# Weight splits of the feed-forward in whole granules without GpSimd's share, and token lists from signs on ScalarE

## The chip, the cores and the metric

The kernel runs on one core of one Trainium2 chip. The metric is the device time of one launch in microseconds (us). The engines are named as the profile names them: PE is TensorE, DVE is VectorE, ACT is ScalarE, POOL is GpSimd, SP is SyncE, which issues most of the DMAs. "L0" and "L1" below are the two layers of the model, while L88 or L343 is a line of the kernel's file.

## What is computed

A diffusion backbone of two layers over 1024 tokens of 1024 channels. Each layer has a mixer (a gated DeltaNet with pooling in the first, a short convolution in the second) and then a feed-forward with 16 experts, in which each expert chooses its 128 tokens. The change touches the feed-forward alone:

```python
def expert_choice_ffn(h, router, w_gate, w_up, w_down):
    b, n, _ = h.shape                                   # 1, 1024
    cap = EC_CAPACITY_FACTOR * n // N_EXPERTS           # 2 * 1024 // 16 = 128
    aff = jax.nn.softmax(jnp.einsum('bnd,de->bne', h, router).astype(jnp.float32), axis=-1)
    gate, idx = lax.top_k(aff.transpose(0, 2, 1), cap)  # each expert's 128 best tokens
    bidx = jnp.arange(b)[:, None, None]
    xg = h[bidx, idx]
    hid = jax.nn.silu(jnp.einsum('becd,edf->becf', xg, w_gate)) * jnp.einsum('becd,edf->becf', xg, w_up)
    y = jnp.einsum('becf,efd->becd', hid, w_down) * gate[..., None].astype(h.dtype)
    return jnp.zeros_like(h).at[bidx, idx].add(y)
```

An expert's weights are two matrices of 1024 x 512 and one of 512 x 1024, all float32: 6 MB an expert, 96 MB a layer.

## The kernel before

**Weights.** Products are made in three passes with operands split into a high part (float32r) and a low part. Weights come from DRAM in granules of 1 MB, 128 partitions x 4 x 512 = 2048 columns. For each granule ACT copies the raw float32 to the high part (whi, L87) and DVE or POOL subtracts to get the low part (wlo, L88). `Weights.split` does so in two halves of 1024 columns, and hands every sixth half to POOL (`pool_share=6`), the others to DVE. An expert has six granules: gate and up for each half of its inputs, then two of down. There are 8 buffers for raw granules and 6 pairs for split ones, taken in turns; SP issues the next load once a raw buffer is free.

**Selection.** `Moe.select` finds each expert's 128th best value by ten rounds of a search. In a round DVE counts on all 1024 tokens (junk), compares (ok, L303), PE sums over partitions (pn, L305), and DVE sets the new candidate; in the first seven rounds this takes an addition of two columns of SBUF (cbase, L308) beside it. Then dg (L315), pth and th spread the threshold, m (L322, L323) marks the tokens above it and equal to it, and 16 matmuls into pp count the marks ahead of each token: one with a triangular matrix, seven with ones for the tiles of tokens ahead, and eight that add the total of the greater ones to the equal ones. Two DVE operations make slot of it, each token's place in each expert's list, or 0.

**Lists and rows.** `Moe.gather` makes an expert's list: a one-hot oh of 8 tiles x 128 places on DVE (L343), eight matmuls of it with the tokens' numbers (pi, L351), a copy to int32 on ACT (idx, L354), then POOL issues the indirect DMA that gathers the rows (xg, L356), and ACT copies the expert's weight of each row out of them (aff, L359). Rows are transposed by PE and split by ACT and DVE (xh, xl).

**Experts.** `Moe.experts` gathers for three experts ahead, prefetches six granules behind the selection, up to four of them with the subtraction on POOL (behind `self.routed`, the last tile's softmax) and the rest on DVE (behind `self.placed`, the last list made so far), then loops over the 16 experts: gather for the third next one, products with gate and up (gu, L139 to L141), silu and product, products with down (py), the result times its weight (y, L454), and an indirect DMA on POOL's queue that adds it to acc in DRAM (L459).

The stage of the experts runs in L0 from the selection at 707.6 us to the last y at 1079.4, in L1 from 1494.9 to 1875.9. What goes on which engine is written in the code; the order of instructions on each engine is set by the scheduler of the framework from priorities, dependences and modelled times, not by the order of the code.

## Time and profile before

| | |
|---|---|
| device time, median of 3 runs | 1914.73 us (1910.54 to 1923.18) |
| span of the profiled execution | 1906.9 us, 26387 instructions |
| PE busy | 1669.8 us (88%) |
| DVE busy | 1373.4 us (72%) |
| ACT busy | 843.1 us (44%) |
| POOL busy | 689.6 us (36%) |
| moved by DMA | 443.73 MB, 233 GB/s in the mean |
| splits on DVE (L88), all shapes | 370, 511.9 us |
| splits on POOL (L88), all shapes | 90, 244.8 us |

The profiled execution has no time of its own beside its span; the span is 7.8 us shorter than the median of the runs. Shares of busy time are means over the whole program. The feed-forward takes about 40% of it, in two stretches, and is read by itself in the rows below.

### The profile page before, as it was taken

The numbers are of one execution on the slowest core, as the hardware profiler recorded it, in microseconds if no ns is written. First come the engines' busy times: TensorE is split into PE (matmuls) and PEld (weight loads), VectorE is DVE, ScalarE is ACT, GpSimd is POOL, SyncE is SP. The second block draws the span as 40 slices with busy tenths as digits, with TensorE's granted clock in tenths as the row PEclk, the third lists the DMA queues.
The fourth block names the chain that finished last, engine by engine and source line by source line (L and its number), as shares of the span: only waits on it lengthen the run. The fifth ranks groups of instructions, "written<-read, shape, count | busy, mean of one in ns | idle before, by whom it ended". The sixth has DMA issues, their size and how long they took to land. (4 is left out here: it accounts for less than half of the span.)

```text
span 1906.9 us, 26387 instructions
## 1 busy us (share of the span) xinstructions
PE 1669.8 (88%) x9561; PEld 1352.4 (71%) x9561; DVE 1373.4 (72%) x2128; ACT 843.1 (44%) x1503; POOL 689.6 (36%) x614
## 2 busy tenths in 40 slices
PE   5999996989979874999998899999999388999995
PEld 3988774767867663777776677888888267777673
DVE  4637777666887866999988858523635688888896
ACT  3644332425642333677665451111222256566673
POOL 3310377551240344444442360000022546454423
PEclk8999998979989886999999999999999689999998
DMA  7425774558768946999998648403354479999975
GB/s 293 135 96 185 229 197 140 149 176 248 241 224 275 349 174 211 333 372 352 349 357 278 209 137 321 132 20 127 133 186 142 176 239 315 350 320 336 349 254 198
DMA packets 261400, 443.73 MB, mean 233 GB/s; under 512 B 46521, under 2 KB 108714, under 8 KB 257174
## 3 DMA queue, kind: packets, MB, share of 16 engines
q1 hardware_dynamic: 252198, 408.76, 62.1%
q0 software_dynamic: 9072, 33.30, 7.2%
q8 instruction: 75, 1.23, 0.3%
q14 instruction: 55, 0.45, 0.1%
HBM read 368.65 MB, written 73.35 MB: 232 GB/s over the span
## 5 line engine op out<-in xcount | busy, mean ns | idle before, releaser
L88 DVE TENSOR_TENSOR wlo<-raw,whi 128x1024 fp32r<-128x1024 f32 (+2 forms) x370 | 511.9, 1426 | 59.1 <-ACT whi L87 59.0
L87 ACT CAST whi<-raw 128x1024 fp32r<-128x1024 f32 (+2 forms) x460 | 438.5, 1021 | 213.4 <-PE pin L140 77.7
L88 POOL TENSOR_TENSOR wlo<-raw,whi 128x1024 fp32r<-128x1024 f32 (+1 forms) x90 | 244.8, 2730 | 337.2 <-ACT whi L87 310.2
L140 PE MATMUL gu<-wlo,xh 128*128 128x512 f32 x512 | 210.3, 411 | 22.8 <-DVE wlo L88 18.7
L139 PE MATMUL gu<-whi,xh 128*128 128x512 f32 x512 | 207.7, 410 | 7.2 <-ACT whi L87 7.1
L141 PE MATMUL gu<-whi,xl 128*128 128x512 f32 x512 | 206.5, 405 | 0.0
L141 PE MATMUL pin<-h1T,wlo 128*128 128x512 f32 x384 | 150.2, 392 | 0.7 <-POOL wlo L88 0.7
L140 PE MATMUL pin<-h1T,whi 128*128 128x512 f32 x384 | 150.7, 393 | 0.0
L139 PE MATMUL pin<-h1T,whi 128*128 128x512 f32 x384 | 148.9, 395 | 0.0
L459 POOL DMA_INDIRECT acc<-y,idx x31 | 85.3, 2750 | 149.6 <-DVE y L454 133.2
L140 PEld LDWEIGHTS gu<-wlo,xh 128*128 128x128 f32 x512 | 99.3, 194 | 53.2 <-DVE wlo L88 26.0
L139 PEld LDWEIGHTS gu<-whi,xh 128*128 128x128 f32 x512 | 99.4, 194 | 32.9 <-ACT whi L87 10.0
L141 PEld LDWEIGHTS gu<-whi,xl 128*128 128x128 f32 x512 | 98.9, 193 | 21.7
L449 PE MATMUL py<-whi,hh 128*128 128x512 f32 x256 | 108.0, 422 | 4.7 <-ACT idx L354 2.6
L785 DVE SCALAR_TENSOR_TENSOR adsum<-raw,cs,adsum 128x512 f32<-128x512 f32 (+1 forms) x77 | 96.6, 1255 | 21.4 <-DMA raw<-in_ada_w_dram 21.0
L449 PE MATMUL py<-wlo,hh 128*128 128x512 f32 x256 | 107.0, 418 | 0.0
L139 PE MATMUL pq<-hT,whi 128*128 128x512 f32 (+1 forms) x256 | 97.7, 382 | 1.8 <-ACT last L1079 1.3
L139 PE MATMUL po<-whi,mh 128*128 128x512 f32 x224 | 92.2, 413 | 6.6 <-DVE ox L611 6.6
L141 PE MATMUL pq<-hT,wlo 128*128 128x512 f32 (+1 forms) x256 | 97.5, 381 | 0.0
L140 PE MATMUL pq<-hT,whi 128*128 128x512 f32 (+1 forms) x256 | 97.0, 379 | 0.0
L140 PE MATMUL po<-wlo,mh 128*128 128x512 f32 x224 | 91.3, 408 | 5.8 <-DVE wlo L88 5.8
L141 PE MATMUL po<-whi,ml 128*128 128x512 f32 x224 | 90.8, 406 | 0.0
(385 smaller groups left out, 3652.4 us busy)
## 6 DMA issues: line engine op xcount, KB each, us to landing
raw<-in_w_gate_dram SPq DMA_DIRECT2D x64, 1024.0 KB
raw<-in_w_up_dram SPq DMA_DIRECT2D x64, 1024.0 KB
raw<-in_w_down_dram SPq DMA_DIRECT2D x64, 1024.0 KB
raw<-in_ada_w_dram SPq DMA_DIRECT2D x32, 1024.0 KB
raw<-in_ada_w_dram SPq DMA_DIRECT2D x64, 256.0 KB
raw<-in_sc_w_in_dram SPq DMA_DIRECT2D x12, 1024.0 KB
table<-h SPq DMA_DIRECT2D x16, 520.0 KB
raw<-in_ev_w_in_dram SPq DMA_DIRECT2D x16, 512.0 KB
```

Source lines behind the costliest of these rows:

```text
L87: nc.scalar.copy(hi[:, part], raw[:, part])
L88: (lo_engine or e).tensor_sub(lo[:, part], raw[:, part], hi[:, part])
L139: nc.tensor.matmul(out, lhs[0], rhs[0], start=start, stop=False)
L140: nc.tensor.matmul(out, lhs[0], rhs[1], start=False, stop=False)
L141: nc.tensor.matmul(out, lhs[1], rhs[0], start=False, stop=stop)
L449: nc.tensor.matmul(py, hh[:, k, :], g[w][:, k, :], start=k == w == 0, stop=False)
L459: self.scattered = nc.gpsimd.indirect_dma_start(out=self.acc[:, :], out_offset=bass.IndirectOffsetOnAxis(ap=idx, axis=0), in_=y, in_offset ...
L785: nc.vector.scalar_tensor_tensor(st["sum"], raw, cs[:, k, 0:1], st["sum"], op0=ALU.mult, op1=ALU.add)
```

## The change

The feed-forward's weights are split in one piece of 2048 columns a granule (`parts=1`), and no piece goes to POOL by turn (`pool_share=0`). The prefetch that names POOL as its engine still goes there. The two other users of `Weights` in this stretch of the program (the early prefetch in layer 0, the output projection in layer 1) keep halves.

The lists are no longer made from slots. With the count of an expert's chosen tokens up to and with each token, a place p of the list belongs to the first token whose count is over p. So the number of the token at place p is the number of tokens whose count is not over p, and that is a sum of signs: ACT takes, for each of the 8 tiles of tokens, the sign of (p + 0.5 - count) with the count as its bias per partition, PE sums the signs over tokens by products with a column of ones, and ACT makes 0.5 x sum + 512 of it, the token's number. Counts are of the greater tokens plus the equal ones up to what is left of the 128 places. That takes the total of the greater ones (pg, eight matmuls of 16 columns), in place of the eight matmuls that added it to the equal ones, and three DVE operations on small tiles in place of two. The counts overwrite the affinities' tile (`self.before = aff`), and `self.placed` is now the last of those three operations.

```diff
 class Weights:
-    def __init__(self, co, raw, pool, size=GRAN, pool_share=6):
+    def __init__(self, co, raw, pool, size=GRAN, pool_share=6, parts=2):
 ...
+        self.parts = parts
 ...
-        n = raw.shape[1] // 2
-        for part in (slice(0, n), slice(n, 2 * n)):
+        n = raw.shape[1] // self.parts
+        for part in (slice(i * n, (i + 1) * n) for i in range(self.parts)):
 def route_constants(co, c, tmp):
-    co.iota1 = c.tile([P, P], F16, name="iota1")
-    nc.gpsimd.iota(co.iota1, pattern=[[1, P]], base=1, channel_multiplier=0, ...)
-    co.tokid = c.tile([P, NT], F16, name="tokid")
-    nc.gpsimd.iota(co.tokid, pattern=[[P, NT]], base=0, channel_multiplier=1, ...)
+    co.places = c.tile([P, P], F16, name="places")
+    nc.gpsimd.iota(co.places, pattern=[[1, P]], base=0, channel_multiplier=0, ...)
+    nc.vector.tensor_scalar(co.places, co.places, 0.5, None, op0=ALU.add)
 ...
+    co.ones16 = c.tile([P, 1], F16, name="ones16")
+    nc.vector.memset(co.ones16, 1.0)
 class Moe:
     def select(self, pool, ps):
 ...
+        pg = ps.tile([P, 512], F32, tag="tr", name=co.name("pg"))
+        for t in range(NT):
+            nc.tensor.matmul(pg[:, :NE], co.one16, m[:, 0, t, :], start=t == 0, stop=t == NT - 1)
         nc.tensor.matmul(pp[:, : 2 * NT * NE], co.tri16, m.rearrange("p m t e -> p (m t e)"), start=True, stop=False)
         for j in range(1, NT):
-            nc.tensor.matmul(pp4[:, :, j:, :], co.one16, m[:, :, : NT - j, :], start=False, stop=False)
-        for t in range(NT):
-            nc.tensor.matmul(
-                pp4[:, 1], co.one16, m[:, 0, t : t + 1, :].to_broadcast([P, NT, NE]), start=False, stop=t == NT - 1
-            )
-        self.slot = self.rp.tile([P, NT, NE], F16, name=f"slot{self.li}")
-        s1 = pool.tile([P, 2, NT, NE], F32, tag="junk", name=co.name("s1"), bufs=1)
-        nc.vector.tensor_tensor(s1, pp4, m, op=ALU.mult)
-        nc.vector.tensor_tensor(self.slot, s1[:, 0], s1[:, 1], op=ALU.add)
+            nc.tensor.matmul(pp4[:, :, j:, :], co.one16, m[:, :, : NT - j, :], start=False, stop=j == NT - 1)
+        left = pool.tile([P, 1, NE], F32, tag="left", name=co.name("left"), bufs=1)
+        nc.vector.tensor_scalar(left[:, 0, :], pg[:, :NE], -1.0, float(CAP), op0=ALU.mult, op1=ALU.add)
+        equal = pool.tile([P, NT, NE], F32, tag="junk", name=co.name("equal"), bufs=1)
+        nc.vector.tensor_tensor(equal, pp4[:, 1], left.to_broadcast([P, NT, NE]), op=ALU.min)
+        self.before = aff
+        self.placed = nc.vector.scalar_tensor_tensor(
+            flat(self.before), pp[:, : NT * NE], -1.0, flat(equal), op0=ALU.mult, op1=ALU.subtract
+        ).ins
     def gather(self, e, pool, ps):
         oh = pool.tile([P, NT, P], F16, tag="oh", name=co.name("oh"), bufs=2)
-        self.placed = nc.vector.tensor_tensor(
-            oh, self.slot[:, :, e : e + 1].to_broadcast([P, NT, P]),
-            co.iota1.rearrange("p (o s) -> p o s", o=1).to_broadcast([P, NT, P]), op=ALU.is_equal,
-        ).ins
         pi = ps.tile([P, 512], F32, tag="tr", name=co.name("pi"))
         for t in range(NT):
-            nc.tensor.matmul(pi[:, :1], oh[:, t, :], co.tokid[:, t : t + 1], start=t == 0, stop=t == NT - 1)
+            nc.scalar.activation(oh[:, t, :], co.places, AF.Sign, bias=self.before[:, t, e : e + 1])
+            nc.tensor.matmul(pi[:, :1], oh[:, t, :], co.ones16, start=t == 0, stop=t == NT - 1)
 ...
-        nc.scalar.copy(idx, pi[:, :1])
+        nc.scalar.activation(idx, pi[:, :1], AF.Copy, scale=0.5, bias=float(SEQ // 2))
 def feed_forward(li, ready, start, before_last):
-            weights = Weights(co, Cycle((raws_on, n_raw), *(...)), Cycle(*splits))
+            weights = Weights(co, Cycle((raws_on, n_raw), *(...)), Cycle(*splits), pool_share=0, parts=1)
```

The changed file's line numbers are higher by one to five. Three places of the order show what moved. The numbers behind tiles' names count tiles; "x8" is eight instructions in a row. First ACT, in layer 0, from the last granule that is prefetched (raw_7479) to the first expert's rows. Before:

```order
L87 CAST whi_7866<-raw_7479 128x1024 x2
L354 CAST idx_7790<-pi_7781 128x1
L354 CAST idx_7807<-pi_7798 128x1
L354 CAST idx_7824<-pi_7815 128x1
L359 COPY aff_7791<-xg_7793 128x1
L133 CAST xh_7835<-pt_7830 128x512
```

And with the change (raw_7480 is the same granule, aff_6918 holds the counts):

```order
L88 CAST whi_7884<-raw_7480 128x2048
L353 ACTIVATE oh_7782<-places,aff_6918 128x128 x8
L353 ACTIVATE oh_7806<-places,aff_6918 128x128 x8
L357 ACTIVATE idx_7800<-pi_7783 128x1
L353 ACTIVATE oh_7830<-places,aff_6918 128x128 x8
L357 ACTIVATE idx_7824<-pi_7807 128x1
L353 ACTIVATE oh_7888<-places,aff_6918 128x128 x8
L357 ACTIVATE idx_7848<-pi_7831 128x1
L353 ACTIVATE oh_8022<-places,aff_6918 128x128 x7
L362 COPY aff_7801<-xg_7803 128x1
L353 ACTIVATE oh_8022<-places,aff_6918 128x128
L134 CAST xh_7859<-pt_7854 128x512
```

The first list's copy to idx stands behind the signs of two experts, and the first copy out of a gathered row behind those of five.

Second POOL, from the end of the last tile's modulation (h, on both) through the prefetch to the first scatter. Before:

```order
L284 TENSOR_TENSOR h_7644<-h_7644,bc_6889 128x1024
L88 TENSOR_TENSOR wlo_7849<-raw_7293,whi_7848 128x1024 x2
L88 TENSOR_TENSOR wlo_7855<-raw_7295,whi_7854 128x1024 x2
L88 TENSOR_TENSOR wlo_7861<-raw_7387,whi_7860 128x1024 x2
L88 TENSOR_TENSOR wlo_7867<-raw_7479,whi_7866 128x1024 x2
L356 DMA xg_7793<-table_73,idx_7790 128x1040
L356 DMA xg_7810<-table_73,idx_7807 128x1040
L356 DMA xg_7827<-table_73,idx_7824 128x1040
L356 DMA xg_7886<-table_73,idx_7883 128x1040
L88 TENSOR_TENSOR wlo_8059<-raw_8056,whi_8058 128x1024
L88 TENSOR_TENSOR wlo_8234<-raw_8231,whi_8233 128x1024
L356 DMA xg_8013<-table_73,idx_8010 128x1040
```

And with the change:

```order
L285 TENSOR_TENSOR h_7645<-h_7645,bc_6890 128x1024
L89 TENSOR_TENSOR wlo_7873<-raw_7294,whi_7872 128x2048
L89 TENSOR_TENSOR wlo_7877<-raw_7296,whi_7876 128x2048
L89 TENSOR_TENSOR wlo_7881<-raw_7388,whi_7880 128x2048
L89 TENSOR_TENSOR wlo_7885<-raw_7480,whi_7884 128x2048
L359 DMA xg_7803<-table_73,idx_7800 128x1040
L359 DMA xg_7827<-table_73,idx_7824 128x1040
L359 DMA xg_7851<-table_73,idx_7848 128x1040
L359 DMA xg_7909<-table_73,idx_7906 128x1040
L359 DMA xg_8043<-table_73,idx_8040 128x1040
L462 DMA acc_75<-y_7992,idx_7800 1024x1024
```

The four prefetched granules stay on POOL, in four pieces where there were eight; the single pieces between the gathers are gone.

Third DVE, from the end of the search (dg) to the first splits of the loop. Before:

```order
L315 TENSOR_SCALAR dg_7744<-ident,cand_7678 128x16
L319 COPY th_7748<-pth_7746 128x16
L322 TENSOR_TENSOR m_7750<-aff_6917,th_7748 128x128
L323 TENSOR_TENSOR m_7750<-aff_6917,th_7748 128x128
L336 TENSOR_TENSOR s_7771<-pp_7753,m_7750 128x256
L337 TENSOR_TENSOR slot_7770<-s_7771 128x128
L343 TENSOR_TENSOR oh_7779<-slot_7770,iota_6503 128x1024
L343 TENSOR_TENSOR oh_7796<-slot_7770,iota_6503 128x1024
L343 TENSOR_TENSOR oh_7813<-slot_7770,iota_6503 128x1024
L343 TENSOR_TENSOR oh_7872<-slot_7770,iota_6503 128x1024
L343 TENSOR_TENSOR oh_7999<-slot_7770,iota_6503 128x1024
L134 TENSOR_TENSOR xl_7836<-pt_7830,xh_7835 128x512
```

And with the change:

```order
L316 TENSOR_SCALAR dg_7745<-ident,cand_7679 128x16
L320 COPY th_7749<-pth_7747 128x16
L323 TENSOR_TENSOR m_7751<-aff_6918,th_7749 128x128
L324 TENSOR_TENSOR m_7751<-aff_6918,th_7749 128x128
L336 TENSOR_SCALAR left_7772<-pg_7755 128x16
L338 TENSOR_TENSOR equal_7774<-pp_7754,left_7772 128x128
L342 SCALAR_TENSOR_TENSOR aff_6918<-pp_7754,equal_7774 128x128
L135 TENSOR_TENSOR xl_7860<-pt_7854,xh_7859 128x512
L135 TENSOR_TENSOR xl_7869<-pt_7863,xh_7868 128x512
L135 TENSOR_TENSOR xl_7918<-pt_7912,xh_7917 128x512
L89 TENSOR_TENSOR wlo_8069<-raw_8066,whi_8068 128x2048
```

Five one-hots are gone between slot and the first rows. The ten rounds ahead of dg, with the seven additions of cbase in them, stand as they did.

## Rows read from the trace of the kernel before

**Rows 1.** Busy time by stretch, the middles of both layers; columns in the first line.

```profile
core 0: us, PE busy (x) PEld busy (x) DVE busy (x) ACT busy (x) POOL busy (x), PEclk, DMA share, GB/s
770.00:1038.00 268.00, 247.09 (x1171) 195.91 (x1170) 252.83 (x215) 176.58 (x228) 116.22 (x52) 0.97 1.01 345
1600.00:1840.00 240.00, 219.72 (x1010) 172.85 (x1009) 214.29 (x187) 151.18 (x194) 114.67 (x45) 0.94 1.00 340
```

**Rows 2.** The same view, four shorter stretches of the middles.

```profile
870.00:920.00 50.00, 48.80 (x237) 38.92 (x235) 48.55 (x44) 34.08 (x44) 18.67 (x9) 1.00 1.04 367
920.00:970.00 50.00, 46.11 (x223) 36.78 (x224) 48.22 (x41) 34.42 (x46) 23.17 (x12) 0.97 1.05 356
...
1600.00:1640.00 40.00, 35.80 (x173) 28.55 (x171) 40.00 (x32) 26.41 (x34) 26.95 (x9) 0.96 1.03 368
1640.00:1680.00 40.00, 37.60 (x172) 29.52 (x173) 29.66 (x31) 22.94 (x29) 13.80 (x7) 0.91 0.91 308
```

**Rows 3.** Groups by line, 747:1080 (layer 0): count, busy, mean ns, idle before.

```profile
L88 DVE TENSOR_TENSOR wlo<-raw,whi 128x1024 fp32r<-128x1024 f32 x152 | 227.3, 1541 | 16.6 <-ACT whi L87 16.6
...
L88 POOL TENSOR_TENSOR wlo<-raw,whi 128x1024 fp32r<-128x1024 f32 x30 | 84.6, 2822 | 125.0 <-ACT whi L87 115.5 <-issue 8.6 <-DVE oh L343 0.8
...
L343 DVE TENSOR_TENSOR oh<-slot,iota 128x1024 f16<-128x1024 f16 x11 | 13.4, 1216 | 2.3 <-PE pi L351 2.3
```

**Rows 4.** The same view, 1533:1876 (layer 1).

```profile
L88 DVE TENSOR_TENSOR wlo<-raw,whi 128x1024 fp32r<-128x1024 f32 x152 | 217.9, 1481 | 15.1 <-ACT whi L87 15.0
...
L88 POOL TENSOR_TENSOR wlo<-raw,whi 128x1024 fp32r<-128x1024 f32 x28 | 83.8, 2995 | 52.2 <-ACT whi L87 35.9 <-issue 15.7 <-PE gu L140 0.4
...
L343 DVE TENSOR_TENSOR oh<-slot,iota 128x1024 f16<-128x1024 f16 x11 | 17.6, 1604 | 5.0 <-PE pi L351 4.9
```

**Rows 5.** Tile wlo, 747:1080: least, median, most ns; first and last start.

```profile
L88 DVE TENSOR_TENSOR wlo<-raw,whi x152: 1207/1214/4466, 753.2 to 1066.9; 128x1024 fp32r<-128x1024 f32 x152
```

**Rows 6.** Timeline (start, length, engine): POOL's pieces of 2048 and 1024 columns.

```profile
544.91 13.91 POOL L95 TENSOR_TENSOR raw<-raw,bc 128x2048 f32<-128x2048 f32 x3
...
549.64 4.82 DVE L134 TENSOR_TENSOR ml<-mt,mh 128x512 fp32r<-128x512 f32 x1
...
820.32 6.74 DVE L88 TENSOR_TENSOR wlo<-raw,whi 128x1024 fp32r<-128x1024 f32 x3
820.74 2.96 POOL L88 TENSOR_TENSOR wlo<-raw,whi 128x1024 fp32r<-128x1024 f32 x1
```

**Rows 7.** Timeline, the selection of layer 0.

```profile
710.15 9.25 POOL L88 TENSOR_TENSOR wlo<-raw,whi 128x1024 fp32r<-128x1024 f32 x4
...
712.01 0.50 DVE L308 TENSOR_TENSOR cbase<-cand,cstep 128x1 f32<-128x1 int32 x1
...
721.19 0.16 DVE L308 TENSOR_TENSOR cbase<-cand,cstep 128x1 f32<-128x1 int32 x1
...
722.87 3.88 ACT L87 CAST whi<-raw 128x1024 fp32r<-128x1024 f32 x4 [16.01 <-DMA table<-h]
...
723.18 0.15 DVE L308 TENSOR_TENSOR cbase<-cand,cstep 128x1 f32<-128x1 int32 x1
...
731.01 2.28 DVE L315 TENSOR_SCALAR dg<-ident,cand 128x16 f32<-128x16 f32 x1
```

**Rows 8.** Timeline, the selection of layer 1.

```profile
1497.47 18.46 POOL L88 TENSOR_TENSOR wlo<-raw,whi 128x1024 fp32r<-128x1024 f32 x8
...
1520.35 0.23 DVE L315 TENSOR_SCALAR dg<-ident,cand 128x16 f32<-128x16 f32 x1
```

**Rows 9.** Timeline, the first lists of layer 0.

```profile
737.61 5.77 DVE L343 TENSOR_TENSOR oh<-slot,iota 128x1024 f16<-128x1024 f16 x5
...
739.30 0.16 ACT L354 CAST idx<-pi 128x1 int32<-128x1 f32 x1 [12.54 <-PE pi L351]
```

**Rows 10.** Timeline, ACT's 128x128 ACTIVATEs with a scale per partition, elsewhere in the program.

```profile
567.77 0.37 ACT L1415 ACTIVATE wd<-psc,g_bed 128x128 f32<-128x128 f32 x1 [4.15 <-PE psc L1412]
568.04 0.36 ACT L1418 ACTIVATE w<-psc,g_bp 128x128 f32<-128x128 f32 x1
```

## What I predict, and why

> **What bounds it now.** I read the stage table first, because the change lives in one stage per layer: the experts, with the selection and the first gathers ahead of them. In the long middle of that stage, 268 us of layer 0 and 240 us of layer 1, three things are nearly full at once [rows 1]. The DMA engines' share is 1.01 and 1.00. VectorE (DVE) is busy for 252.83 of 268 us and 214.29 of 240. [...] The question is which of the three gives way when DVE gets lighter.
>
> Two stretches answer it [rows 2]. In 1640 to 1680 DVE is busy for only 29.66 of 40 us and the layer is no faster for it: the DMA share is 0.91. In 920 to 970 DVE is full (48.22 of 50 us) and DMA is at 1.05, its highest. So DMA has 4 to 5% in hand in the middle, not more, while DVE and PE follow it.
>
> Next I read the groups of instructions. DVE's subtractions of 1024 columns cost 1541 ns on average in layer 0 and 1481 ns in layer 1 [rows 3, 4], but their median is 1214 ns and the longest took 4466 ns [rows 5]. The mean is made by a few that stood still. The timeline shows with whom: GpSimd (POOL) started a subtraction at 820.74 that took 2.96 us, and DVE's three from 820.32 on took 6.74 us instead of 3.6 [rows 6]. An earlier place shows it for POOL's 2048 columns: three take 13.91 us, 4.64 each, and a DVE subtraction of 512 columns begun at 549.64, inside the second, took 4.82 us and ended just behind it [rows 6]. So one waits for the other's whole instruction.
>
> **The change part by part.**
>
> *POOL's share goes to DVE.* POOL made 30 pieces in layer 0's stage and 28 in layer 1's. At 1.214 us DVE's 152 pieces a layer would cost 184.5 us; they cost 227.3 and 217.9, so 42.8 and 33.4 us is standing still. That goes. DVE gets at most 30 x 1.214 = 36.4 and 28 x 1.214 = 34.0 us in return. No row shows DVE's subtraction at 2048 columns: above, twice 1.214; below, as with POOL's 4.64 against two of 2.31 (9.25 / 4, [rows 7]), nothing is saved by width. I take 2.43 us.
>
> *One-hots leave DVE.* In the stage 13.4 and 17.6 us of DVE go [rows 3, 4]. Together DVE loses 42.8 + 13.4 - 36.4 = 19.8 us in layer 0 and 33.4 + 17.6 - 34.0 = 17.0 in layer 1: some 6% of its work. ScalarE (ACT) gets eight signs an expert. The nearest rows are two 128x128 ACTIVATEs with a scale per partition, 0.27 us from start to start and 0.37 us long [rows 10]; bounds 0.20 (the shorter one less any operand) and 0.37, and I take 0.265 as they follow each other. That is 2.1 us an expert, 34 a layer, on an engine busy for 176.58 of 268 us: to about 77%. In the order the signs stand six granules or more ahead of the products that PE makes of them, so they are hidden there; uncovered they would cost PE the 2.1 us. The same counts of table loads stand in both orders.
>
> *What the lighter DVE buys.* If DMA ran at 1.05 throughout, layer 0's middle would shrink by 268 x (1 - 1.01/1.05) = 10.2 us and layer 1's by 240 x (1 - 1.00/1.05) = 11.4. Of the latter 40 x (1 - 0.91/1.05) = 5.3 us was lost where DVE was idle for a quarter of the time, so it isn't DVE's to give. I take 10.2 + 6.1 = 16.3, rounded down to 15, since ACT's longer pieces cost something.
>
> [...] The rows show 368 GB/s in 1600 to 1640 against 345 and 340 in the middles [rows 1, 2]; held all through, that would give 268 x (1 - 345/368) + 240 x (1 - 340/368) = 35 us. [...] My 15 rests on the shares alone.
>
> *The ramp of layer 1.* In its first 67 us POOL's pieces fall on DVE's as elsewhere: 33.4 + (17.6 - 13.4) = 37.6 us of standing still over 343 us is 7 us there. Half of it counts, as PE has six ready granules at first: 4 us. For layer 0 I count nothing, since the first new split also comes later (below).
>
> *The selection gets longer.* This is the cost that the change doesn't speak of. Four granules a layer stay on POOL ahead of the experts, and these become 2048 columns wide too. The ten rounds of the selection run beside them, and each of the first seven has a DVE addition of two SBUF columns (cbase). Undisturbed it takes 0.16 us and rounds follow each other by 1.99 us (721.19, 723.18); inside a POOL piece it waits for the piece's end: begun at 712.01 it took 0.50 us, to 710.15 + 2.31 [rows 7]. Pieces of 2.31 us cost a round 0.3 us. Pieces of 4.63 us stretch a round to 4.63. Layer 0: POOL's first run ends its pieces at 714.8 and 719.4, where the additions of the second and third round get through; the next two come at 721.2 and 723.2. The second run starts when ACT has made 2048 columns, 722.87 + 2.0 = 724.9 at the latest, and its pieces end at 729.5 and 734.1, where the sixth and seventh addition get through. From there to dg it took 731.01 - 723.33 = 7.7 us. dg begins at 741.8 and takes 0.23 us instead of 2.28: 742.1 against 733.3, **+8.8 us**. Layer 1: one run from 1497.47 [rows 8] with ends at 1502.1, 1506.7, 1511.3 and 1515.9, each letting one round through, then two free rounds and 7.7 us: 1527.6 against 1520.35, **+7.3 us**. Nothing covers it: PE and DMA wait for the first gather by then, with all buffers full.
>
> [...]
>
> *The first list.* Before, the first one-hot takes a fifth of 5.77 us, and idx follows at 739.30, 1.7 us after the start [rows 9]. In the order now, idx stands behind two experts' signs on ACT: 16 x 0.265 = 4.2 us, so 4.3 us: **+2.6 us** in each layer (bounds: signs at 0.20 give +1.6, at 0.37 give +4.3). The chain from idx to the first product moves along. Select's three DVE operations, for two, and its eight narrow matmuls change nothing of size. ACT then reads a later expert's row before its first new whi, some 4 us after the old place; PE's six granules hide it.
>
> **Sum.** Start-up +8.8 + 7.3 + 2 x 2.6 = +21.3; middles -15; ramp -4: +2.3 us. The profiled execution spanned 1906.9 us, so 1909.2; the median of the runs stands 7.8 us above that span, which gives **1917 us**. A change under 1%, 19 us, can't be told from none here.
>
> **Rivals.**
> 1. *DVE was the bound alone.* Then the middles go at the best PE pace of the trace: 237 matmuls in 870 to 920 [rows 2] is 4.74 per us, against 1171/268 = 4.37 and 1010/240 = 4.21. The gain is 268 x 0.078 + 240 x 0.112 = 48 us, with the ramp 52, less 21.3: about 1884. DVE's 94% speaks for it, DMA's share against. Chance 0.11.
> 2. *The additions slip through.* If the selection isn't stretched, start-up costs 5.2 and the sum is -13.8, about 1901; with DMA at 1.05 throughout and a ramp of 7 it is -23.4, about 1891. The 4.82 us subtraction speaks against it. Chance 0.15, a third of it beyond 1%.
> 3. *DMA has no more to give (the other side).* The shares count overlapping packets, so 1.01 may be full already. Then nothing pays for the start-up: +21.3, about 1936. It decides once the middles give back under 2 us. For it: DMA stays at 0.99 or more in most stretches. Against: 0.91 and 1.05 beside each other. Chance 0.16.
> 4. *Coarser splits starve PE.* A granule is ready after 2.0 + 2.4 us instead of half of it. If PE's waits for splits (one a granule at worst, 0.4 us each of the 2 us) came on top, +20 more: about 1937. Chance 0.06.
>
> **How the numbers follow.** The forecast, within 1%, has 0.52, and rival 2 adds 0.10 to it: 0.62. Faster by over 1%: rival 1 and a third of rival 2, with a little for start-ups that the rounds' luck shortens, 0.18. Slower: rivals 3 and 4, less those that stop short of 19 us, 0.20. The likeliest case gives 1917. The range of 1891 to 1938 reaches to rival 2's lower and rival 3's upper end and leaves out rival 1, half of rival 4 and little else.
>
> **What would show it.** Right: no POOL subtraction in the middles and DVE's at 2.3 to 2.5 us with hardly a longer one; cbase additions of some 2.7 us in both selections; dg near 742 and 1528 (if what stands ahead starts at the same time); first gu products some 10 us later after the last logits; DMA shares of 1.03 or more with DVE under 90% busy in the middles. Wrong: additions of 0.2 us beside POOL's wide pieces, or middles that shrink by more than 25 us together, or signs far from 0.27 us.

## The result, and the profile after

The changed kernel takes 1888.59 us (median of 4 runs, 1879.51 to 1892.76) against 1914.7: a ratio of 0.9849, with a 95% interval of 0.9817 to 0.9881. That is 1.5% less. The forecast was 1917 us with a range of 1891 to 1938, so the result lies 2.4 us below the range. The profiled execution spans 1877.7 us. Both traces are of the fastest run of their kernel (1910.54 and 1879.51 us), so what follows explains 29.2 us of span where the medians differ by 26.1. Medians and ratios leave out one slow run of 4123.51 us, of b_split_noscat below.

To see where the 29.2 us of span went I cut both traces at the same instructions: the first po (layer 0's output projection), the copy that starts a search (cand), the end of dg, the first idx, the start of the first and the end of the last gu of a layer. Stages between them, in us, worked out from starts and ends in the traces:

| stage | before | after | |
|---|---|---|---|
| up to the first po | 555.0 | 554.0 | -1.0 |
| output projection, to L0's search | 152.8 | 139.6 | **-13.2** |
| L0 search, to dg | 25.4 | 33.1 | +7.7 |
| L0 first list (dg to idx), first rows | 6.0, 8.0 | 8.0, 7.9 | +1.9 |
| L0 experts, first to last gu | 322.5 | 313.6 | **-8.9** |
| L1's mixer, to its search | 425.2 | 428.3 | +3.1 |
| L1 search | 25.5 | 31.6 | +6.1 |
| L1 first list, first rows | 6.0, 6.8 | 8.0, 7.9 | +3.1 |
| L1 experts | 334.3 | 307.6 | **-26.7** |
| to the end | 39.3 | 38.1 | -1.2 |

The forecast had written +8.8 and +7.3 for the searches, +2.6 for each list, and, middles and ramp together, some -9 for layer 0's experts and -10 for layer 1's. Searches, lists and layer 0's experts came so. Layer 1's experts gained more than twice as much, and the output projection, of which the forecast did not speak, gained 13 us.

The groups of layer 0's experts after (742 to 1070) answer to [rows 3]; columns as there:

```profile
L89 DVE TENSOR_TENSOR wlo<-raw,whi 128x2048 fp32r<-128x2048 f32 x90 | 202.8, 2288 | 27.1 <-ACT whi L88 27.0
...
L353 ACT ACTIVATE oh<-places,aff 128x128 f16<-128x128 f16 x89 | 27.4, 396 | 0.0
```

A split of 2048 columns costs 2.29 us, not 2.43, and no longer stands still. A sign takes 0.40 us alone and 0.30 in a row (2.43 us for eight, where 2.1 was written); the forecast's lower bound of 0.20 was an estimate that no row shows.

Busy time by stretch, whole stages from first to last gu: two rows of before, then two of after.

```profile
core 0: us, PE busy (x) PEld busy (x) DVE busy (x) ACT busy (x) POOL busy (x), PEclk, DMA share, GB/s
747.30:1069.80 322.50, 300.52 (x1413) 238.23 (x1412) 294.87 (x257) 210.35 (x271) 126.54 (x58) 0.97 0.93 313
1533.40:1867.60 334.20, 306.61 (x1413) 241.42 (x1412) 290.43 (x257) 210.37 (x271) 151.48 (x56) 0.95 0.91 307
```

```profile
742.70:1056.20 313.50, 297.32 (x1405) 237.51 (x1406) 257.40 (x182) 226.74 (x269) 56.59 (x29) 0.97 0.94 322
1532.00:1839.70 307.70, 295.00 (x1405) 236.50 (x1406) 257.17 (x183) 227.16 (x269) 67.94 (x28) 0.97 0.95 329
```

Read PE's column. It had the same products to make (8 records fewer in each layer after are gaps of the trace, worth up to 1.9 us of busy time), and was idle for 322.50 - 300.52 = 22.0 us before and 16.2 after in layer 0, for 27.6 and 12.7 in layer 1. Its busy time fell too, by 3.2 and 11.6 us; in layer 1 the granted clock beside it rose from 0.95 to 0.97, while in layer 0 both read 0.97. Idle and busy time make up the whole of the gain: 5.8 + 3.2 and 14.9 + 11.6. DVE lost 37.5 and 33.3 us of work.

What PE waited for in layer 1's experts, before and after (us in total, times, longest):

```profile
PE gu L140 <- DVE wlo L88: 7.3, 6, 2.4
...
PE gu L139 <- ACT whi L87: 5.3, 5, 1.9
PE gu L140 <- POOL wlo L88: 4.1, 2, 3.6
```

```profile
PE py L452 <- ACT hh L134: 6.7, 4, 2.7
PE gu L141 <- DVE wlo L89: 4.2, 3, 3.0
PE gu L140 <- ACT whi L88: 1.7, 2, 0.9
```

Waits for splits (whi and wlo) fell from 16.7 to 5.9 us. In layer 0 they hardly fell, from 13.2 to 12.7, but changed their engine: 11.4 us were waits for DVE's low parts before, 10.7 are waits for ACT's high parts after. What layer 0 gained in idle time were the waits for the silu's product (sg on DVE, 6.0 to 2.3 us) and some small ones.

The searches, answering to [rows 7]: tile cbase (least, median, most ns), and the timeline of layer 0's search.

```profile
L309 DVE TENSOR_TENSOR cbase<-cand,cstep x14: 154/2654/4184, 695.0 to 1508.6; 128x1 f32<-128x1 int32 x14
```

```profile
696.05 8.96 POOL L89 TENSOR_TENSOR wlo<-raw,whi 128x2048 fp32r<-128x2048 f32 x2
...
697.91 2.65 DVE L309 TENSOR_TENSOR cbase<-cand,cstep 128x1 f32<-128x1 int32 x1
...
708.45 8.96 POOL L89 TENSOR_TENSOR wlo<-raw,whi 128x2048 fp32r<-128x2048 f32 x2 [3.44 <-ACT whi L88]
...
708.79 4.18 DVE L309 TENSOR_TENSOR cbase<-cand,cstep 128x1 f32<-128x1 int32 x1
...
726.54 0.23 DVE L316 TENSOR_SCALAR dg<-ident,cand 128x16 f32<-128x16 f32 x1
```

The addition begun at 697.91 ends at 700.56, when POOL's first piece of 4.48 us ends (696.05 + 4.48 = 700.53); the one begun at 708.79 ends at 712.97, with the next first piece (712.93). That is the wait of the forecast.

### The profile page after: what moved, and what is told of

Read it like the earlier page. It is cut to its first block, busy times and chain, and to the rows that moved or that the text cites. A ratio compares the mean times of both kernels' runs of the same rounds, so it can differ in the third digit from the quotient of the medians.

```text
span 1877.7 us, 26055 instructions
## 1 busy us (share of the span) xinstructions
PE 1655.3 (88%) x9561; PEld 1344.1 (72%) x9561; DVE 1305.4 (70%) x1975; ACT 897.3 (48%) x1570; POOL 530.7 (28%) x549
## 4 chain that ended last, share of the span: by engine, by line
PE 50%; DVE 13%; DMA 7%; ACT 5%; issue 4%; SPq 2%; POOL 0%; DVEq 0%; ACTq 0%; POOLq 0%
PE py L452 5%; PE gu L141 4%; PE gu L140 4%; PE gu L142 4%; PE pin L140 4%; PE pin L141 4%; PE pin L142 4%; PE po L141 3%; PE po L142 3%; PE po L140 3%; DVE wlo L89 3%; ACT whi L88 3%; PE py L455 2%; DMA raw<-in_w_up_dram 2%; SPq L918 1%
## 5 line engine op out<-in xcount | busy, mean ns | idle before, releaser
L89 DVE TENSOR_TENSOR wlo<-raw,whi 128x2048 fp32r<-128x2048 f32 (+3 forms) x245 | 471.9, 1959 | 82.6 <-ACT whi L88 82.5
L88 ACT CAST whi<-raw 128x2048 fp32r<-128x2048 f32 (+3 forms) x271 | 420.9, 1598 | 213.5 <-PE pin L141 77.7
L89 POOL TENSOR_TENSOR wlo<-raw,whi 128x1024 fp32r<-128x1024 f32 (+2 forms) x26 | 80.6, 3117 | 167.1 <-ACT whi L88 167.0
L353 ACT ACTIVATE oh<-places,aff 128x128 f16<-128x128 f16 x256 | 77.9, 394 | 46.9 <-DVE aff L342 46.9
L359 POOL DMA_INDIRECT xg<-table,idx x32 | 48.8, 1526 | 175.9 <-ACT idx L357 133.1
```

Source lines behind the costliest of these rows:

```text
L88: nc.scalar.copy(hi[:, part], raw[:, part])
L89: (lo_engine or e).tensor_sub(lo[:, part], raw[:, part], hi[:, part])
L353: nc.scalar.activation(oh[:, t, :], co.places, AF.Sign, bias=self.before[:, t, e : e + 1])
L359: nc.gpsimd.indirect_dma_start(out=xg, out_offset=None, in_=self.table[:, :], in_offset=bass.IndirectOffsetOnAxis(ap=idx, axis=0))
```

## The experiments

All kernels are compared with runs of the kernel before on the same chip and hour; two of them may come from different chips, and then differences of a few us between their medians tell nothing. "Stage" means a stage of the table above.

**What moved the output projection.** Nothing of the change lies there but the constants, which are made at its start. `b_const` is the kernel before with

```diff
-    nc.gpsimd.iota(co.iota1, pattern=[[1, P]], base=1, ...)
+    nc.gpsimd.iota(co.iota1, pattern=[[1, P]], base=0, ...)
+    nc.vector.tensor_scalar(co.iota1, co.iota1, 1.0, None, op0=ALU.add)
```

> The kernel before, with one constant made as the change makes its own: the iota starts at 0 and VectorE adds 1 to it. Its order of instructions through layer 0's output projection is then that of the changed kernel, and nothing else of the change is in it. Theory (the scheduler's order in layer 0's output projection, shaken up by the constants, made the selection of layer 0 start 14.2 us earlier): the selection starts near 694 us instead of 707.8, everything behind it keeps its lengths, about 1901 us, ratio 0.993. Rival (the earlier start came from something else of the change, or from luck in one profiled execution): selection at 705 to 710, 1915 us, ratio 1.000.

1900.27 us, ratio 0.9928 (0.9901 to 0.9955). The stage takes 139.1 us; experts (320.5 and 337.0) and searches (25.3 and 25.5) stay within 3 us, while layer 1's mixer takes 431.4 us for 425.2. One addition on DVE (0.19 us for the changed kernel's own, at 559.9) shifts the scheduler's order from there to the search on PE, DVE, ACT, POOL and SP, and again in the experts of both layers, as the traces show. What it avoids shows in the views of 630 to 655: of before, then of the changed kernel, and PE's longest waits of before in 555 to 710 (total, times, longest).

```profile
630.00:655.00 25.00, 21.09 (x112) 18.02 (x111) 21.57 (x28) 9.62 (x23) 10.71 (x6) 0.84 1.03 398
```

```profile
630.00:655.00 25.00, 25.00 (x144) 21.49 (x143) 19.91 (x32) 13.12 (x30) 13.11 (x8) 1.00 1.02 388
```

```profile
PE po L139 <- DVE ox L611: 6.6, 4, 3.9
PE po L140 <- DVE wlo L88: 5.8, 3, 3.8
```

Before, products wait for DVE's sums (ox), once for 3.9 us up to 652.1, and the clock granted behind that wait is 0.50 (652.1 to 655). It is also 0.72 in 636 to 642, where no wait but 32 narrow products of the router (128x16, from 633.3 on) stand ahead; together this makes the 0.84. In the new order PE waits for none of these sums there and keeps 1.00. Over the stage PE's idle time falls from 18.1 to 12.7 us and its busy time from 134.7 to 126.9. It is luck of an order: the scheduler was given nothing that knows of it.

`a_oldconst` is the other half: the changed kernel with the old constants (the half goes into the counts, a column of iota1 serves as ones).

> The changed kernel with the constants of the kernel before (the half that the signs need is put into the counts instead), so that its order up to layer 0's selection is that of the kernel before. Theory (two separate gains, 14.2 us from the order of the output projection and the rest from the experts, less the longer selections): selection of layer 0 at 708 us, layer 1's experts still some 27 us shorter than before, about 1902 us, ratio 0.993. Rival (the earlier start belongs to the splits or the signs): selection near 694 us, 1889 us, ratio 0.985.

1899.67 us, ratio 0.9911 (0.9879 to 0.9944): stage 153.1 us, experts 312.5 and 312.5, searches as in the changed kernel. So the change without the accident of the order is worth 0.9%.

`b_nopool_const` and `b_nopool` (below) are a further pair.

> b_nopool with the constant of b_const: a third pair with and without the new order of layer 0's output projection. Its price stands at 15.7 us by the first pair of medians (before and b_const), 11.1 by the second (a_oldconst and the changed kernel) and 2.2 by the third (b_split and b_split_const). Theory (the stage is 13 us shorter whatever follows): stage of 139 us instead of 153, 1877 us, ratio 0.980. Rival (what is won there is lost again further on where the experts' splits are lighter): stage of 139 us, but 1887 us or more, ratio 0.985 or more.

1872.92 us, ratio 0.9769 (0.9729 to 0.9808), 17.0 us below b_nopool; stage 138.9 instead of 153.3. In the differences of medians the order is worth 15.7 (before and b_const), 11.1 (a_oldconst and the change), 17.0 and, for b_split and b_split_const, 2.2 us. The stage is 151.5 to 153.3 us long in every trace with the old order and 138.9 to 142.3 in every one with the new. In the traces the last pair differs by 16.5 us of span, but b_split's trace is of its slowest run (1891.41 us, the others 1881.86 to 1883.83) and b_split_const's of its fastest (1874.91, the others 1880.82 to 1881.31); why their medians don't show the 13 us stays open.

**What moved the experts.** `b_split` takes the splits of the change alone; the one-hots stay on DVE.

```diff
-            weights = Weights(..., Cycle(*splits))
+            weights = Weights(..., Cycle(*splits), pool_share=0, parts=1)
```

> The kernel before with the feed-forward's splits in whole granules on VectorE, and nothing of the signs: the one-hots stay on VectorE. Theory A (the experts of layer 1 gained 26.7 us because GpSimd's pieces no longer stop VectorE's): experts of layer 1 20 us shorter or more, of layer 0 some 5 us shorter, searches 7 us longer each: about 1904 us, ratio 0.995. Theory B (the one-hots' leaving VectorE made the gain): experts of layer 1 at most 8 us shorter, layer 0's no shorter, searches longer: about 1920 us, ratio 1.003.

1883.1 us, ratio 0.9819 (0.9788 to 0.985): better than either theory had it, and no worse than the whole change, though it has the old order of the output projection. Experts 310.6 and 304.9; searches 33.3 and 31.6. `b_nopool` keeps the halves and only sets pool_share=0.

> The kernel before with GpSimd's share of the feed-forward's splits off and the halves kept: only pool_share=0. Theory A (the experts gained because GpSimd's pieces no longer stop VectorE's): experts of layer 1 by 20 us or more shorter, of layer 0 by 8 or more, searches as before: about 1882 us, ratio 0.983. Theory B (the gain comes from the width: one instruction for two on ScalarE and VectorE): experts within 8 us of before in each layer, about 1912 us, ratio 0.998.

1889.9 us, ratio 0.9864 (0.9825 to 0.9902); experts 311.2 and 319.8, searches 25.8 and 25.5. Against before, POOL's leaving alone gives 11.3 us in layer 0 and 14.5 in layer 1. Against b_split, the width would give another 14.9 in layer 1, but b_nopool_const, with halves too, has experts of 309.7 and 308.5, so that is not the width's (more on it below). The width of POOL's prefetched pieces costs the searches 7.5 and 6.1.

`a_halves` has the signs without the new splits: the changed kernel less `pool_share=0, parts=1`.

> The changed kernel with the weight splits of the kernel before (halves, every sixth on GpSimd): what is left of the change is the signs and the constants with their order of the output projection (13 us less). Theory (the signs cost time: 2 us for each layer's first list and some in the experts, where ScalarE is fuller): 1908 us or more, ratio 0.996 or more. Rival (one-hots off VectorE help the experts as much as they cost): about 1900 us or less, ratio 0.992 or less.

1924.6 us, ratio 1.006 (1.0035 to 1.0085), although it has the lucky order; b_const, with one-hots on DVE, had 0.9928. Experts 337.7 and 332.1 against b_const's 320.5 and 337.0. PE's longest waits in its experts of layer 0, and in b_const's:

```profile
PE gu L141 <- DVE wlo L89: 21.4, 10, 3.4
```

```profile
PE gu L140 <- DVE wlo L88: 8.3, 8, 3.3
```

DVE was lighter (279.1 us of work against b_const's 290.2) and yet its splits came later. ACT makes the high part ahead of each low part and had 24 us more to do; that the delay starts there is argued from this, not shown. Layer 1's experts were 4.9 us shorter than b_const's, so the loss stands in layer 0 and in the lists.

`b_split_const` is the changed kernel with one-hots for signs.

> The changed kernel with the one-hots on VectorE instead of the signs: b_split with the constant of b_const, so that the order up to layer 0's selection is that of the changed kernel. Theory (the signs cost some 14 us: 2 us for each first list, the rest in the experts, and the order of the output projection is worth 13 us by itself): 13 us off b_split, about 1869 us, ratio 0.976. Rival (signs cost nothing, and the two differ by chance): 1886 us, ratio 0.985.

1880.93 us, ratio 0.9815 (0.9769 to 0.9861). The signs therefore cost 7.7 us here (1888.59 - 1880.93, not clear of noise: the intervals overlap), 16.6 in the pair a_oldconst and b_split, and 24.3 in the pair a_halves and b_const. Of this, 2 us a list stand in the stages; the rest is in the experts. The two halves of the change pull in opposite ways: splits gain, signs lose.

**All experts side by side.** Each edit also draws a new order of instructions in the experts, so that one pair of kernels can't tell an edit from its order. The kernels together can (us, layer 0 and layer 1; a_cpsum and best0 come below):

| kernel | POOL takes each sixth half | DVE's pieces | lists from | experts |
|---|---|---|---|---|
| before | yes | 1024 | one-hots | 322.5, 334.3 |
| b_const | yes | 1024 | one-hots | 320.5, 337.0 |
| a_halves | yes | 1024 | signs | 337.7, 332.1 |
| b_nopool | no | 1024 | one-hots | 311.2, 319.8 |
| b_nopool_const | no | 1024 | one-hots | 309.7, 308.5 |
| b_split | no | 2048 | one-hots | 310.6, 304.9 |
| b_split_const | no | 2048 | one-hots | 313.3, 303.5 |
| best0 | no | 2048 | one-hots | 312.6, 305.1 |
| the change | no | 2048 | signs | 313.6, 307.6 |
| a_oldconst | no | 2048 | signs | 312.5, 312.5 |
| a_cpsum | no | 2048 | signs | 314.9, 316.8 |

b_split, b_split_const and best0 have the same order on PE, DVE and ACT in layer 1's experts, and these take 303.5 to 305.1 us. b_nopool and b_nopool_const, which differ by the constant far ahead, have different orders there, and 11.3 us between them: that is what an order can be worth in one layer. POOL's leaving stands clear of that: with POOL's share the experts take 320.5 to 337.7 us in layer 0 and 332.1 to 337.0 in layer 1, without it 309.7 to 314.9 and 303.5 to 319.8. The signs show less clearly, in the sum of both layers: 621 to 632 us in the three kernels that have them, against 615 to 618 in the three with one-hots and the same splits. The width of DVE's pieces does not show: b_nopool_const and best0 differ in it alone (ACT's pieces go with DVE's), and both have sums of 618 us, at 1872.92 and 1869.86 us.

What POOL's leaving does shows on the chain of work that ended last (from the last instruction back, at each step to what released it), through layer 1's experts. DVE's low parts hold 23.3% of the stage before and 20.2% in b_const, 7.2% in b_nopool and 6.2% in b_nopool_const, while PE's work rises from 51% and 57% to 71% and 73%.

**Whether the DMA engines bound the experts**, as the forecast had it. `b_split_noscat` leaves out 22 of b_split's 31 scatters, the experts that the expectation lists:

```diff
+            if e % 4 != 3 and e < NE - 2:
+                continue
             self.scattered = nc.gpsimd.indirect_dma_start(
```

> b_split with 22 of its 31 scatters left out (experts 0 to 2, 4 to 6, 8 to 10, 12 and 13 of each layer): the sum lacks these experts, all other work stands. A scatter is 128 packets of 4096 B of about 359 ns, some 2.9 us of all 16 DMA engines. Theory (with whole-granule splits the DMA engines set the pace of the experts, 20.4 us each): the experts shorten by 1.7 us or more for each scatter left out, down to PE's 18.6 us each, about 40 us in all: 1843 us, ratio 0.962. Rival (PE with its waits for splits sets the pace): less than 10 us, 1875 us, ratio 0.979.

Ratio 0.9876 (0.984 to 0.9912), some 1892 us: not faster than b_split. The kernel was run once more for its trace.

> The kernel of b_split_noscat again, for its trace: 22 of 31 scatters are left out, the sum lacks those experts. Its time was not below that of b_split, so either the DMA engines did not set the experts' pace, or what they have to spare is lost to waits of PE. Theory (DMA follows): experts of 311 and 305 us as in b_split, at a DMA share of 0.9 or less, with PE's share of its time unchanged. Rival (the gain is there and given back elsewhere): experts shorter by 10 us or more in one of the layers, and another stage longer.

1891.18 us in a single run. Whole stages of b_split, then of this trace:

```profile
761.40:1072.10 310.70, 295.30 (x1407) 236.75 (x1406) 269.41 (x193) 202.24 (x181) 74.90 (x29) 0.97 0.95 325
1543.40:1848.30 304.90, 291.26 (x1390) 233.43 (x1390) 269.46 (x193) 202.28 (x181) 61.39 (x29) 0.97 0.97 337
```

```profile
757.40:1067.50 310.10, 296.41 (x1413) 237.17 (x1412) 270.50 (x195) 202.70 (x181) 47.72 (x18) 0.97 0.87 307
1539.90:1851.80 311.90, 297.69 (x1406) 236.57 (x1406) 269.44 (x193) 202.54 (x181) 32.41 (x18) 0.97 0.87 311
```

The DMA share fell from 0.95 and 0.97 to 0.87, at the same pace or a slower one (the 7 us of layer 1 are within what an order is worth). With the new splits DMA follows; PE, 95% busy in both, leads.

> The kernel before with the same 22 of 31 scatters left out (the sum lacks those experts): the forecast's own step, that the DMA engines had 4 to 5% in hand and then bound the experts, tested on the kernel for which it was made. If DMA bound them: the DMA share of the middles stays near 1.0, and the experts shorten by about the 63 us of DMA time that is taken away, down to PE's pace of some 300 us a layer: some 50 us less, 1863 us, ratio 0.974. If it did not (theory now: PE waits for splits, and DMA follows): the share falls to 0.93 or less at the same pace, experts within 8 us of 322 and 334 us, ratio 0.995 to 1.003.

For the kernel before the answer is mixed: 1892.75 us, ratio 0.9875 (0.9823 to 0.9928), experts 313.9 and 319.3 at a share of 0.86 and 0.87. Neither expectation holds. It gained 24 us, half of what a DMA bound would give, while b_split gained nothing at a higher share. Other rows of the trace of before speak against a DMA bound. A load that comes late would hold up ACT's copy to the high part, and in the experts of layer 0 all such waits were these two, 7.1 us:

```profile
ACT whi L87 <- DMA raw<-in_w_gate_dram: 4.3, 3, 3.6
ACT whi L87 <- DMA raw<-in_w_down_dram: 2.8, 1, 2.8
```

In layer 1 they were 2.6 us, and loads of weights held 4.4% of the chain through its experts. What before and b_split differ in is POOL's queue, which in before holds both the scatters and a sixth of the splits. The timeline of before, layer 1, shows what that does (POOL, then ACT, then DVE):

```profile
1699.18 7.99 POOL L459 DMA_INDIRECT acc<-y,idx  x1 [9.96 <-DVE y L454]
1706.64 2.95 POOL L88 TENSOR_TENSOR wlo<-raw,whi 128x1024 fp32r<-128x1024 f32 x1
...
1711.55 2.43 POOL L88 TENSOR_TENSOR wlo<-raw,whi 128x1024 fp32r<-128x1024 f32 x1
```

```profile
1701.23 2.00 ACT L87 CAST whi<-raw 128x1024 fp32r<-128x1024 f32 x2
```

```profile
1706.23 4.46 DVE L88 TENSOR_TENSOR wlo<-raw,whi 128x1024 fp32r<-128x1024 f32 x1
```

And busy time by stretch of the same place, with PE's two waits there (timeline):

```profile
1690.00:1697.00 7.00, 5.65 (x26) 3.98 (x24) 7.00 (x9) 2.94 (x5) 0.00 (x0) 1.00 1.05 396
1697.00:1700.00 3.00, 1.12 (x13) 0.92 (x14) 3.00 (x5) 3.00 (x4) 0.82 (x1) 0.74 1.05 387
1700.00:1705.30 5.30, 5.30 (x13) 4.14 (x14) 5.30 (x6) 3.23 (x6) 5.30 (x1) 0.50 1.05 385
1705.30:1712.00 6.70, 6.70 (x33) 5.43 (x32) 5.98 (x4) 0.59 (x1) 6.52 (x4) 1.00 1.07 335
```

```profile
1697.04 0.66 PE L435 MATMUL pt<-ident,sg 128*128 128x128 f32 x4 [1.21 <-DVE sg L432]
...
1699.81 0.80 PE L139 MATMUL gu<-whi,xh 128*128 128x512 f32 x1 [1.84 <-ACT whi L87]
```

A scatter's issue held POOL for 7.99 us. Two splits queued behind it (a gather's issue lies between them) began at 1706.64 and 1711.55, while ACT's last high part ahead of them had been made at 1703.23. POOL's piece then held up DVE's, which the profile dates 0.4 us earlier, at 1706.23: 4.46 us for 1.21, to 1.1 us behind POOL's end. The rows of PE show what these waits cost beyond themselves: in the second of the two, of 1.21 and 1.84 us, the clock granted falls to 0.50 and stays there to 1705.3; behind that it is 1.00 again. Products of 512 columns start 0.43 us apart in that stretch and 0.23 us apart behind it, so the 13 that take 5.30 us would take some 3.0. By this estimate the 3.05 us of waiting cost another 2.3. That fewer scatters in POOL's queue gave b_noscat its gain is argued from this, and from b_split's getting nothing; no run has the scatters on another queue, and 8.6 and 15.0 us in the two layers are near what an order can be worth.

**Whether POOL's wide pieces stretch the search.** `a_cpsum` is the changed kernel with the constant of cbase added by PE, so that the new candidate needs one column of SBUF:

```diff
-                nc.vector.tensor_tensor(base, cand, co.cstep[:, r : r + 1], op=ALU.add)
-                nc.vector.tensor_scalar(cand, pn[:, :1], step, base, op0=ALU.mult, op1=ALU.add)
+                nc.vector.scalar_tensor_tensor(cand, pn[:, :1], step, cand, op0=ALU.mult, op1=ALU.add)
 ...
+                nc.tensor.matmul(pn[:, :1], wd, co.one16[:, :1], start=True, stop=False)
```

> The changed kernel with the search's cbase addition gone: PE adds the constant into pn with a second one-column product, and VectorE makes the new candidate from PSUM and one SBUF column. GpSimd's wide pieces beside the search stay. Theory (the additions of two SBUF columns wait for GpSimd's whole pieces, and nothing else of the search does): rounds of about 1.9 us beside the pieces, the search some 20 us long in both layers instead of 33.2 and 31.6, so about 24 us off, 1865 us, ratio 0.974. Rival (whatever reads SBUF on VectorE waits, or the search waits for something else): searches of 30 us or more, 1889 us, ratio 0.985.

1884.07 us, ratio 0.9816 (0.9781 to 0.9851); searches 26.2 and 25.0. The first seven rounds follow each other by 1.93 us beside POOL's 4.48 us pieces. The operations on cand of this kernel (least, median, most ns):

```profile
L315 DVE SCALAR_TENSOR_TENSOR cand<-pn,cand x14: 157/158/159, 708.4 to 1503.6; 128x1 int32<-128x1 f32 x14
L318 DVE CUSTOM_DVE_ANT_0 cand<-cand,delta x6: 158/1298/3697, 722.1 to 1513.7; 128x2 uint16<-128x2 uint16 x6
```

The one with PSUM and one SBUF input did not wait in any of its 14 (159 ns at most); the integer additions of the last three rounds, with two, now meet the pieces that cbase met before, up to 3.7 us. So the mechanism stands, and 7 us a layer came off instead of 12, because a freed search runs its last rounds into the same pieces. Of these 13.5 us the median shows only 4.5; in the trace the experts, 1.3 and 9.2 us longer in a new order, take most of the rest back.

**Put together.** `best0` is b_split_const with the prefetched granules split in halves on POOL again.

> b_split_const with the prefetched granules in halves on GpSimd. Theory (GpSimd's wide pieces stretch the search by 7.9 us in layer 0 and 6.1 in layer 1): searches of 25.5 us again, 14 us off b_split_const, about 1856 us, ratio 0.969. Rival (the experts wait for something else by then): as b_split_const.

1869.86 us, ratio 0.976 (0.9714 to 0.9806); searches 25.3 and 25.5: 11 us off b_split_const, where 14 were expected. `best1` adds the search of a_cpsum.

> Whole-granule splits on VectorE as in b_split, one-hots on VectorE, and three more things: the constant of b_const (its order of layer 0's output projection), the search without the cbase addition as in a_cpsum, and the granules prefetched on GpSimd in halves again. If the parts add up: 13 us off b_split by the order, and searches of 22 us or less in both layers instead of 33.4 and 31.7, some 21 us more: about 1850 us, ratio 0.965. If they don't (the experts then start earlier only to wait for weights): 1870 us or more.

1861.36 us, ratio 0.9734 (0.9701 to 0.9767), not 1850; searches 25.1 and 23.4. What was left in layer 0 were waits at the scaled identity (1.16 us), an addition (1.54) and dg (2.28). `best2` takes quarters of 512 columns on POOL and the plain identity.

> As best1, with the prefetched granules in quarters of 512 columns on GpSimd, and the constant of the search by a product with the identity instead of a scaled one. Theory (what is left of the waits in best1's search is for one piece of GpSimd's each: 1.0 us at the scaled identity, 1.4 to 1.8 at the last additions, 2.05 at dg): searches of 21 us in both layers, 4 us off best1, about 1857 us, ratio 0.971. Rival (other order of the output projection, more ScalarE pieces): 1865 us or more.

1859.28 us, ratio 0.9704 (0.9659 to 0.975); searches 22.7 and 22.1. It is 1.5% below the changed kernel by their ratios, some 28 us: its splits without its signs, without wide pieces beside the search, and with the order of the output projection as it fell.

## Why the prediction was wrong

**The search and the lists: right.** The searches grew by 7.7 and 6.1 us for 8.8 and 7.3, by the mechanism that was named: cbase's median is 2.65 us (2.7 was written), and a_cpsum takes the waits away with the additions. Rival 2 falls. In a_cpsum the operation with PSUM and one SBUF column, in their place, took 157 to 159 ns in all 14, five of which began beside POOL's wide pieces in layer 0 (707.92 to 716.89). Lists cost 2.0 us each for 2.6.

**What lies ahead of the selection: counted at nothing without a word.** The step that went wrong stands in "if what stands ahead starts at the same time": the order was compared only from the selection on, and no term of the sum had what lies ahead. It had changed from layer 0's output projection on, for 13 us in the trace.

**What the lighter DVE buys: wrong in size and in kind.** This is the step that cost most: the sum had -15 for the middles and -4 for the ramp, and the experts gained 35.6 us. DVE lost 37.5 and 33.3 us where 19.8 and 17.0 were worked out. Twice 1.214 us was taken for the wide piece, which takes 2.29 (2288 ns in the mean of 90), and each piece was priced at its own length though pieces in a row overlap (b_nopool: 180 pieces, 1216 ns each, busy for 209.8 us and not 218.9). Then the gain was capped by the DMA share, 1.05 at most. noscat_look refutes the cap for the new splits: with the share at 0.87 nothing gets faster. For the splits of before the short waits for loads (7.1 and 2.6 us) speak against it, and b_noscat leaves part of it open. The rows that were read as the DMA's giving way (0.91 in 1640 to 1680, where DVE was idle) had PE busy for 37.60 of 40 us at a granted clock of 0.91: it was PE that was full. In layer 1 this cost most: 5.3 us were struck out "where DVE was idle", and the ramp was given 4; its experts gained 26.7 in this trace, and 17.5 and 21.8 in those of a_cpsum and a_oldconst, with the same splits and lists.

**What was missing** was the price of PE's waits. PE was 93 and 92% busy, nearest to its own limit. Idle time of 22.0 and 27.6 us stood in the trace, waits for splits above all (13.2 and 16.7), and a clock of 0.50 behind a wait of 1.84 us in the timeline above. [rows 1] gave the clock, 0.97 and 0.94, but no term used it. Rival 1, whose 1884 us came nearest, had PE's best pace as the limit; its condition, DVE alone as the bound, is not what the runs show: on the chain through layer 1's experts DVE's low parts held 23% before and PE's work 51%, and in b_nopool DVE is still busy for 276.8 of 311.2 us and the gain is there. In the timeline above POOL's part of the splits was late itself and made DVE's late. Rival 3, a DMA that is full already, falls, since the experts did gain. Rival 4 falls too, since PE's idle time shrank in both layers; its 20 us was no product of the figures beside it, as 192 granules at 0.4 us would be 77.

**The signs: wrong.** "Hidden" was argued from their place in the order, and DVE's relief by the one-hots was booked as a gain. Three pairs have signs dearer by 7.7 (within noise) to 24.3 us. The engine they went to is the one that every split begins on: PE's waits for ACT's high parts in layer 0 are 9.6 to 10.7 us in the three kernels with signs and whole granules, and none in b_split, b_split_const and best0. In layer 1 both kinds have such waits, of 0.6 to 7.7 us.

So 1889 is no single effect: by the trace -13 from an order, +19 from searches, lists and first rows, -36 from the experts, in which the signs' cost is contained.

## What to carry to other kernels

Where one engine is nearest to its limit (PE, 93 and 92% busy here), price a change by that engine's waits and by the clock that the trace shows behind them (0.50 for 5.3 us here), not by the busy share of those that feed it. Compare the order of the whole program, since a constant can move 13 us far from the change. Where each edit draws a new order, put a gain down to an edit only when several kernels with and without it agree. And test a supposed DMA bound by taking bytes away: a share near 1 that falls at the same pace (0.95 to 0.87 in layer 0 here) was no bound.

## What the runs showed of the hardware

Beside POOL's pieces DVE's operations differed in what they waited for: PSUM and one SBUF column, for nothing (157 to 159 ns in all 14, a_cpsum); two SBUF columns, up to the end of the piece (2.65 us in the median, 4.18 at most, for 0.15 undisturbed, in the changed kernel); but also a plain scaling of SBUF by a column (dg, 2.28 us for 0.23 in best1), while the counting pass with its accumulator kept 1.28 us throughout (a_cpsum). The issue of a scatter on POOL took 1.54 to 7.99 us (before), and the split queued behind the longest one began 7.5 us after it. 380 GB/s were held for 40 us (b_split, 1680 to 1720), and 398 for 25 us (before, 630 to 655).
